# Fifteen tiny router-logit loads on the scalar queue of a two-group top-2 dispatch kernel

## The chip, the cores and the metric

The kernel runs on one core of one Trainium2 chip. The metric is the device time of one execution in microseconds (us), the median over several runs. In the profile, DVE is the vector engine, ACT the scalar engine, POOL GpSimd, and SP the sync engine; SPq and ACTq are the instruction queues from which the sync and scalar engines issue transfers. Sixteen DMA engines move the data for both; q1 holds what SP issued, q10 what ACT issued.

## What is computed

Sixteen batches of 1024 tokens give 16384 rows of 512 float32 numbers. Each row has eight router logits. The softmax over the eight is cut to its two largest, these two are scaled to sum to one, and the row is written twice, once times each weight:

```python
    topk_indices = np.argsort(probs, axis=-1)[..., -k:]
    topk_probs = np.take_along_axis(probs, topk_indices, axis=-1)
    topk_probs = topk_probs / np.sum(topk_probs, axis=-1, keepdims=True)
    x_expanded = x[:, :, np.newaxis, :].repeat(k, axis=2)
    return (x_expanded * topk_probs[..., np.newaxis]).astype(np.float32)
```

Of two logits that differ by d, the weights are sigmoid(-d) and sigmoid(d), so neither exponentials nor a division is needed. The work is almost all movement: 33.6 MB of x in, 67.1 MB out.

## The kernel before, in words

The 16384 rows are laid over 128 partitions, 128 rows in each, and cut in two groups of 65 and 63 rows (`GROUPS`). The tile `xs` has 65 places for rows; `osp` has 18 places for pairs of output rows. Group 0 is loaded in pieces of 6, 28 and 31 rows, group 1 in pieces of 4, 28 and 31 (`LOADS`). Where the text says "28-row load" or "31-row load" it means the one of group 1, unless it says otherwise.

The logits come behind the first piece (lines 144 and 145), and `top2_weights` turns all of them into the weights `WA` by a small tournament on DVE and two sigmoids on ACT. Then each group is multiplied out in the pieces of `STORES`: some into `osp`, others in place, into the part of `xs` whose rows are already used up. The multiplications are DVE passes (line 164), but for the last four rows of group 1's first piece, which ACT makes (line 157). Each piece is stored by line 176.

Loads and stores all go out on SP in the order of the program, but for two on ACT: the first store of group 0, and the 4-row load of group 1, which the text calls the late load. The late load stands behind a pause: line 128 copies two rows onto themselves on ACT, and is made to wait until the fourth of group 0's five stores has landed. The fifth store of group 0 (16 rows out of `xs`) is called the last store below. The 28-row load and the 31-row load follow on SP.

Every transfer reports its landing on one of eight completion counters. The framework deals the counters out in turn in the order of the program, and a transfer that takes a counter again waits, before it is issued, until the transfer that held the counter before has landed. In the program as built before the change the order and the counters are: first load 0, the two logit loads 1 and 2, group 0's 28 rows 3, the store on ACT 4, group 0's 31 rows 5, the other four stores of group 0 on 6, 7, 0 and 1 (the last store has 1), the late load 2, the 28-row load 3, the 31-row load 4, and the four stores of group 1 on 5, 6, 7 and 0. The 28-row load waits for counter 7 (a store that has read the rows it overwrites); the 31-row load waits for counter 1, the last store, for the same reason.

Of the kernel before, what the change touches and what calls it, by code (L numbers as in the profile page):

```python
# [1 line left out]

# [4 lines left out]

F32 = mybir.dt.float32
ALU = mybir.AluOpType
ACTF = mybir.ActivationFunctionType  # L10
P = 128


def top2_weights(nc, WA, dlt, room, logits, E):

    tt = nc.vector.tensor_tensor
    hi, lo, n = None, None, E  # L20
    while n > 1:
        n //= 2
        if hi is None:
            a, b = logits[:, :, 0:n], logits[:, :, n : 2 * n]
            nhi, nlo = room(n), b
            tt(nhi, a, b, op=ALU.max)  # L26
            tt(nlo, a, b, op=ALU.min)  # L27
        else:
            a, b = hi[:, :, 0:n], hi[:, :, n : 2 * n]
            nhi, nlo, tmp = room(n), room(n), room(n)  # L30
            tt(tmp, lo[:, :, 0:n], lo[:, :, n : 2 * n], op=ALU.max)  # L31
            tt(nlo, a, b, op=ALU.min)  # L32
            tt(nlo, nlo, tmp, op=ALU.max)  # L33
            tt(nhi, a, b, op=ALU.max)  # L34
        hi, lo = nhi, nlo
    tt(dlt, hi[:, :, 0], lo[:, :, 0], op=ALU.subtract)  # L36
    nc.scalar.activation(WA[:, :, 0], dlt, ACTF.Sigmoid, scale=-1.0)  # L37
    nc.scalar.activation(WA[:, :, 1], dlt, ACTF.Sigmoid, scale=1.0)  # L38

GROUPS = [65, 63]

LOADS = [[6, 28, 31], [4, 28, 31]]
BASE = [0, 1]

STORES = [
    [(0, 3, "osp", 0), (3, 15, "osp", 3), (18, 16, "xs", 0), (34, 15, "osp", 0), (49, 16, "xs", 33)],
    [(0, 16, "osp", 2), (16, 16, "xs", 0), (32, 15, "osp", 0), (47, 16, "xs", 32)],
]  # L50

L = 18

FREE = [3, 2]

ACT_ROWS = 4


@with_exitstack
def kernel(  # L60
    ctx: ExitStack,
    tc: tile.TileContext,
    x: bass.AP,
    router_logits: bass.AP,
    k: bass.AP,
    out: bass.AP,
):
    nc = tc.nc
    B, S, D = x.shape
    E = router_logits.shape[-1]  # L70
    N = B * S
    assert int(k) == 2 and E == 8 and N == P * sum(GROUPS)
    M = N // P

    x_v, o_v, rl_v = [], [], []
    t0 = 0
    for n in GROUPS:
        t1 = t0 + P * n
        x_v.append(
            x.rearrange("b s d -> (b s) d")[t0:t1].rearrange("(p m) d -> p m d", p=P)  # L80
        )
        o_v.append(
            out.rearrange("b s k d -> (b s) k d")[t0:t1].rearrange(
                "(p m) k d -> p m k d", p=P
            )
        )
        rl_v.append(
            router_logits.rearrange("b s e -> (b s) e")[t0:t1].rearrange(
                "(p m) e -> p m e", p=P
            )  # L90
        )
        t0 = t1

    wpool = ctx.enter_context(tc.tile_pool(name="wpool", bufs=1))
    xs = wpool.tile([P, max(GROUPS), D], F32)
    osp = wpool.tile([P, L, 2, D], F32)
    WA = wpool.tile([P, M, 2], F32)
    dlt = wpool.tile([P, M], F32)


    flat = osp.rearrange("p l k d -> p (l k d)")
    taken = [0]

    def room(n):
        o = taken[0]
        taken[0] += M * n
        return flat[:, o : o + M * n].rearrange("p (m n) -> p m n", n=n)

    logits = room(E)

    def place(where, at, n):

        if where == "osp":
            return osp[:, at : at + n]
        return xs[:, at : at + 2 * n, :].rearrange("p (r k) d -> p r k d", k=2)

    m0 = 0
    stores = []
    for g, G in enumerate(GROUPS):
        x0, r = BASE[g], 0  # L120
        for n in LOADS[g]:

            late = g == 1 and r == 0
            if late:


                rows = xs[:, x0 : x0 + 2, :]
                pause = nc.scalar.activation(rows, rows, ACTF.Copy)  # L128
                tc.add_manual_dep(
                    pause.ins,  # L130
                    stores[-2].ins.name,
                    mybir.DependencyInfo(
                        mybir.DependencyClass.Sync, mybir.DependencyReason.DATA
                    ),
                    reason="begin when the store ahead of the last has landed",
                )
                tc.keep_in_program_order(pause)
            queue = nc.scalar if late else nc.sync
            load = queue.dma_start(xs[:, x0 + r : x0 + r + n, :], x_v[g][:, r : r + n, :])  # L139
            tc.keep_in_program_order(load)  # L140
            r += n
            if g == 0 and r == 6:
                n0 = GROUPS[0]
                tc.keep_in_program_order(nc.sync.dma_start(logits[:, :n0], rl_v[0]))  # L144
                tc.keep_in_program_order(nc.sync.dma_start(logits[:, n0:], rl_v[1]))  # L145
                top2_weights(nc, WA, dlt, room, logits, E)
        assert r == G
        for r, n, where, at in STORES[g]:
            og = place(where, at, n)

            again = where == "osp" and at == 0 and r > 0
            cuts = [0, FREE[g], n] if again else [0, n]
            if g == 1 and r == 0:
                cuts = [0, n - ACT_ROWS]
                for j in range(n - ACT_ROWS, n):
                    for k2 in range(2):
                        nc.scalar.activation(  # L157
                            og[:, j, k2, :],
                            xs[:, x0 + r + j, :],
                            ACTF.Copy,  # L160
                            scale=WA[:, m0 + r + j, k2 : k2 + 1],
                        )
            for a, b in zip(cuts, cuts[1:]):
                nc.vector.tensor_tensor(  # L164
                    og[:, a:b],
                    xs[:, x0 + r + a : x0 + r + b, :]
                    .unsqueeze(2)
                    .to_broadcast([P, b - a, 2, D]),
                    WA[:, m0 + r + a : m0 + r + b, :]
                    .unsqueeze(3)  # L170
                    .to_broadcast([P, b - a, 2, D]),
                    op=ALU.mult,
                )

            queue = nc.scalar if g == r == 0 else nc.sync
            stores.append(queue.dma_start(o_v[g][:, r : r + n], og))  # L176
            tc.keep_in_program_order(stores[-1])
        m0 += G


# [1 line left out]
_INS = ['x', 'router_logits', 'k']  # L182
_OUTS = [((16, 1024, 2, 512), 'float32')]

_NUMBERS = {'k': 2}


# [26 lines left out]
```

## Time and profile before

| what | value |
|---|---|
| median of 3 runs | 239.71 us (239.71 to 239.82) |
| span of the profiled execution | 238.1 us |
| what lies around the span, against the median | 1.6 us |
| bytes moved | 101.19 MB, mean 425 GB/s |
| DVE busy, ACT busy | 137.6 us, 7.9 us |

The profile gives no time of its own for the profiled execution beside its span; the 1.6 us are the median less that span. In the view by windows the columns are the stretch in us from the start of the span, its length, the busy time of DVE, ACT and POOL with their instructions, the granted TensorE clock, the share of the stretch for which the DMA engines were busy, and GB/s. A packet there is counted where it starts, so a share over 1 only means that packets that start in the stretch run on past its end.

### The profile page before, as it was taken

What the parts mean: (1) busy time and instruction counts of PE and PEld (TensorE: products, weight loads), DVE (VectorE), ACT (ScalarE), POOL (GpSimd) and SP (SyncE); (2) the same over time, 40 slices, a digit from 0 to 9 for tenths busy, and PEclk for the clock granted to TensorE, in tenths of its full rate; (3) what the DMA queues carried; (4) which work ended last, traced back from release to release, by engine and by line L of the source; (5) the groups of instructions that cost most, each with busy time, mean ns of one, the idle gap of its engine ahead of it and who ended that gap; (6) DMA issues with size and microseconds to landing.
All of it is one profiled execution on the core that took longest, in us unless ns stands there. A gap on an engine that the chain in (4) does not pass through costs nothing.

```text
span 238.1 us, 115 instructions
## 1 busy us (share of the span) xinstructions
DVE 137.6 (58%) x22; ACT 7.9 (3%) x12; POOL 0.2 (0%) x4
## 2 busy tenths in 40 slices
DVE  0560499999789999100000009999936999950000
ACT  2000000000000000010000007000000000000000
POOL 0000000000000000000000000000000000000000
DMA  7979998979998999989999899898989989979894
GB/s 262 533 337 519 430 418 374 496 341 495 462 396 374 506 433 392 495 352 483 486 396 417 376 479 501 352 506 363 517 363 451 429 363 495 485 341 517 352 528 176
DMA packets 2448, 101.19 MB, mean 425 GB/s; under 512 B 272, under 2 KB 400, under 8 KB 528
## 3 DMA queue, kind: packets, MB, share of 16 engines
q1 hardware_dynamic: 2160, 98.57, 96.1%
q10 hardware_dynamic: 288, 2.62, 2.6%
HBM read 34.08 MB, written 67.11 MB: 425 GB/s over the span
## 4 chain that ended last, share of the span: by engine, by line
DMA 50%; DVE 38%; SPq 1%; issue 0%; DVEq 0%
DMA xs<-in_x_dram 30%; DVE osp L164 24%; DMA out_dram<-osp 20%; DVE xs L164 14%; SPq L144 0%; SPq L145 0%; SPq L139 0%; SPq L176 0%; DVEq L164 0%
## 5 line engine op out<-in xcount | busy, mean ns | idle before, releaser
L164 DVE TENSOR_TENSOR osp<-xs,WA 128x3072 f32<-128x3072 f32 (+4 forms) x7 | 65.1, 9298 | 65.6 <-DMA xs<-in_x_dram 56.8
L164 DVE TENSOR_TENSOR xs<-xs,WA 128x16384 f32<-128x16384 f32 x4 | 68.9, 17225 | 0.2
L157 ACT ACTIVATE osp<-xs,WA 128x512 f32<-128x512 f32 x8 | 5.0, 708 | 37.6 <-DMA xs<-in_x_dram 37.6
L26 DVE TENSOR_TENSOR osp<-osp 128x512 f32<-128x512 f32 x1 | 0.7, 692 | 8.4 <-DMA osp<-in_router_logits_dram 8.4
L128 ACT ACTIVATE xs<-xs 128x1024 f32<-128x1024 f32 x1 | 1.1, 1056 | 90.8 <-DMA out_dram<-osp 90.8
L37 ACT ACT_TABLE_LOAD x1 | 1.3, 1283 | 0.7 <-PEq L195 0.7
L27 DVE TENSOR_TENSOR osp<-osp 128x512 f32<-128x512 f32 x1 | 0.7, 691 | 0.0
L32 DVE TENSOR_TENSOR osp<-osp 128x256 f32<-128x256 f32 (+1 forms) x2 | 0.7, 350 | 0.0
L31 DVE TENSOR_TENSOR osp<-osp 128x256 f32<-128x256 f32 (+1 forms) x2 | 0.7, 350 | 0.0
L33 DVE TENSOR_TENSOR osp<-osp 128x256 f32<-128x256 f32 (+1 forms) x2 | 0.7, 350 | 0.0
L34 DVE TENSOR_TENSOR osp<-osp 128x256 f32<-128x256 f32 (+1 forms) x2 | 0.7, 348 | 0.0
L37 ACT ACTIVATE WA<-dlt 128x128 f32<-128x128 f32 x1 | 0.3, 317 | 10.3 <-DVE dlt L36 10.3
L36 DVE TENSOR_TENSOR dlt<-osp 128x128 f32<-128x128 f32 x1 | 0.3, 292 | 0.0
L38 ACT ACTIVATE WA<-dlt 128x128 f32<-128x128 f32 x1 | 0.3, 299 | 0.0
L195 POOL MEMSET const-bfloat16-1.0<- 128x1 bf16 x1 | 0.1, 102 | 0.0
L195 POOL MEMSET const-uint8-127<- 128x1 uint8 x1 | 0.1, 102 | 0.0
L195 POOL MEMSET const-float32-1.0<- 128x1 f32 x1 | 0.1, 99 | 0.0
L195 POOL MEMSET const-float32-0.0<- 128x1 f32 x1 | 0.1, 98 | 0.2 <-issue 0.2
## 6 DMA issues: line engine op xcount, KB each, us to landing
out_dram<-osp SPq DMA_DIRECT2D x3, 7680.0 KB, 23.4
xs<-in_x_dram SPq DMA_DIRECT2D x2, 7936.0 KB, 40.9
xs<-in_x_dram SPq DMA_DIRECT2D x2, 7168.0 KB, 35.2
xs<-in_x_dram SPq DMA_DIRECT2D x1, 1536.0 KB, 6.2
out_dram<-osp ACTq DMA_DIRECT2D x1, 1536.0 KB, 24.7
xs<-in_x_dram ACTq DMA_DIRECT2D x1, 1024.0 KB, 24.8
osp<-in_router_logits_dram SPq DMA_DIRECT2D x1, 260.0 KB, 6.4
osp<-in_router_logits_dram SPq DMA_DIRECT2D x1, 252.0 KB, 6.6
```

The costliest lines, as they stand in the source:

```text
L26: tt(nhi, a, b, op=ALU.max)
L27: tt(nlo, a, b, op=ALU.min)
L31: tt(tmp, lo[:, :, 0:n], lo[:, :, n : 2 * n], op=ALU.max)
L32: tt(nlo, a, b, op=ALU.min)
L33: tt(nlo, nlo, tmp, op=ALU.max)
L34: tt(nhi, a, b, op=ALU.max)
L36: tt(dlt, hi[:, :, 0], lo[:, :, 0], op=ALU.subtract)
L37: nc.scalar.activation(WA[:, :, 0], dlt, ACTF.Sigmoid, scale=-1.0)
L128: pause = nc.scalar.activation(rows, rows, ACTF.Copy)
L157: nc.scalar.activation(og[:, j, k2, :], xs[:, x0 + r + j, :], ACTF.Copy, scale=WA[:, m0 + r + j, k2 : k2 + 1],)
L164: nc.vector.tensor_tensor(og[:, a:b], xs[:, x0 + r + a : x0 + r + b, :] .unsqueeze(2) .to_broadcast([P, b - a, 2, D]), WA[:, m0 + r + a : ...
L195: nc = _bacc.Bacc("TRN2", target_bir_lowering=False, num_devices=1)
```

## The change

A tile `probe` is added, 15 slots of 20 numbers in each partition. Right behind the late load, fifteen loads are added on the ACT queue. Load number n reads the first 4 + n numbers of each of the first n rows of the router logits, laid as 128 rows of 1024 numbers, into slot n - 1 of `probe`: one row of 20 bytes in the first, fifteen rows of 76 bytes in the last, 120 rows and 6880 bytes in all. Nothing reads `probe`. They are called tiny loads 1 to 15.

```diff
     dlt = wpool.tile([P, M], F32)
+    probe = wpool.tile([P, 15, 20], F32)
...
             queue = nc.scalar if late else nc.sync
             load = queue.dma_start(xs[:, x0 + r : x0 + r + n, :], x_v[g][:, r : r + n, :])
             tc.keep_in_program_order(load)
+            if late:
+                rows2 = router_logits.rearrange("b s e -> (b s e)").rearrange(
+                    "(p m) -> p m", p=P
+                )
+                for n2 in range(1, 16):
+                    w = 4 + n2
+                    tc.keep_in_program_order(
+                        nc.scalar.dma_start(probe[:n2, n2 - 1, :w], rows2[:n2, :w])
+                    )
```

In the program as built the instructions of DVE, POOL and PE stay as they were, and so do SP's transfers and their order. On ACT the fifteen loads stand between the late load and the eight copies of line 157. In the program's order they stand ahead of the 28-row and the 31-row load, so they take fifteen turns of the counters: tiny loads 1 to 7 have counters 3, 4, 5, 6, 7, 0 and 1, tiny load 8 has 2, tiny loads 9 to 15 have 3 to 7, 0 and 1. The 28-row load now has counter 2, the 31-row load 3, and the four stores of group 1 have 4 to 7. The waits for the holder before are, as built:

| transfer | queue | counter | waits for |
|---|---|---|---|
| tiny load 1, 2, 3, 4 | ACT | 3, 4, 5, 6 | transfers of group 0 ahead of its last three stores |
| tiny load 5, 6 | ACT | 7, 0 | nothing more (the pause has waited for both) |
| tiny load 7 | ACT | 1 | the last store |
| tiny load 8 | ACT | 2 | the late load |
| tiny loads 9 to 15 | ACT | 3 to 7, 0, 1 | tiny loads 1 to 7 |
| 28-row load | SP | 2 | tiny load 8, and counter 7 as before |
| 31-row load | SP | 3 | tiny load 9, and the last store as before |
| stores of group 1 | SP | 4 to 7 | tiny loads 10 to 13, and what they waited for before |

The eight copies of line 157 and the first DVE pass of group 1 wait for the 28-row load under its new counter.

## Prediction

> **What bounds the kernel now.** I read the page's busy slices and queues first, then the chain of waits, then the timeline around the late load.
>
> ```profile
> DVE 137.6 (58%) x22; ACT 7.9 (3%) x12; POOL 0.2 (0%) x4
> ...
> DMA  7979998979998999989999899898989989979894
> ...
> DMA packets 2448, 101.19 MB, mean 425 GB/s; under 512 B 272, under 2 KB 400, under 8 KB 528
> ...
> q1 hardware_dynamic: 2160, 98.57, 96.1%
> q10 hardware_dynamic: 288, 2.62, 2.6%
> ```
>
> The DMA engines are the bound: 96.1% + 2.6% of their time is taken, no slice stands below 7 but the tail, and DVE has 42% to spare. What leaves the engines empty anywhere in the middle therefore comes out at the end. What merely adds bytes costs next to nothing when the bytes are 6880 of 101 million.
>
> ```profile
> 96.78 45.47 DMA xs<-in_x_dram
> 142.25 0.03 issue
> 142.27 0.05 DVEq L164
> 142.32 0.04 issue
> 142.37 12.97 DVE osp L164
> ...
> 194.61 17.23 DVE xs L164
> ```
>
> In the chain of waits the 28-row load is issued at 96.78 and holds the chain until 142.25, when the first DVE pass of group 1 is let go. All that ends the program hangs on that landing.
>
> ```profile
> 96.39 0.33 SPq L176 DMA_DIRECT2D out_dram<-xs  x1
> 96.78 28.30 SPq L139 DMA_DIRECT2D xs<-in_x_dram  x2
> 103.64 1.06 ACT L128 ACTIVATE xs<-xs 128x1024 f32<-128x1024 f32 x1 [90.84 <-DMA out_dram<-osp]
> 104.73 0.34 ACTq L139 DMA_DIRECT2D xs<-in_x_dram  x1
> 142.32 5.01 ACT L157 ACTIVATE osp<-xs,WA 128x512 f32<-128x512 f32 x8 [37.62 <-DMA xs<-in_x_dram]
> 142.37 12.96 DVE L164 TENSOR_TENSOR osp<-xs,WA 128x12288 f32<-128x12288 f32 x1 [46.00 <-DMA xs<-in_x_dram]
> ```
>
> The timeline shows why the early issue matters. The last store goes out at 96.39, the 28-row load 0.4 us later, long before the store's data have left: its data lie in the queue behind the store's. The 31-row load, the second of the two in the 28.30, had to wait for the last store to land:
>
> ```profile
> SPq L139 <- DMA out_dram<-xs: 26.9, 1, 26.9
> ...
> L139 SPq DMA_DIRECT2D xs<-in_x_dram x5: 340/441/965, 0.7 to 124.7; - x5
> ```
>
> The last issue of that line starts at 124.7, so that is when the last store's landing is known. The late load is known to have landed 24.8 us (its row of DMA issues, below) after 104.73, at 129.5.
>
> **The change part by part.** Added are fifteen issues on ACT, 120 rows, and a changed dealing of the counters. Three things have to be priced.
>
> *The issues.* ACT issues the late load in 0.34 us; the five of SP on line 139 take 0.340 to 0.965. Fifteen take 5.1 us by the first figure, 14.5 by the last. ACT has nothing to do from 105.07 until 142.32 (37.62 idle in the row above), so the issuing as such is hidden; without that cover it would cost those 5 to 14 us.
>
> *The rows.* Three stretches of the DMA view, after the last store's final packets, price small packets:
>
> ```profile
> DMA packets 64, 1.18 MB, mean 590 GB/s; under 512 B 16, under 2 KB 16, under 8 KB 16
> ...
> q1 hardware_dynamic: 32, 0.92, 106.2%
> q10 hardware_dynamic: 32, 0.26, 30.9%
> ...
> q1 hardware_dynamic: 16, 0.92, 68.3%
> q10 hardware_dynamic: 16, 0.13, 10.0%
> ...
> q1 hardware_dynamic: 16, 0.92, 264.5%
> q10 hardware_dynamic: 16, 0.00, 1.1%
> ```
>
> They are 123.5 to 125.5, 125.5 to 128.6 and 128.6 to 129.4. In the last, 16 packets on 16 engines fill 1.1% of 0.8 us: 9 ns for a completion packet. The 16 of 57,344 bytes beside them take 264.5% of 0.8 us, 2.12 us each. The busiest engine gets at most 15 tiny rows and 15 completions; at 9 ns that is 0.3 us, and it is spread over a stretch in which the engines are empty anyway, as comes next. I take 0, at most 0.3.
>
> *The waits.* This decides. The 28-row load now waits on SP for tiny load 8; tiny load 8 stands on ACT behind tiny load 7, which waits for the last store, and itself waits for the late load. So the 28-row load can't be issued at 96.8 any more, but only when the last store and the late load have landed and a tiny load has made its round trip. By then q1 and q10 are empty. Behind the waiting instruction on SP stand the 31-row load and all of group 1's stores; for them wait DVE, and ACT with line 157. Behind tiny load 7 on ACT stand tiny loads 8 to 15 and the eight copies.
>
> Step by step, in us from the start:
>
> 1. Last store known landed: 124.7. Its path before that is untouched. Tiny load 7 is issued, 0.34, until 125.1.
> 2. Late load landed. The three stretches show q1 and q10 taking turns packet by packet: between the last store's 16 completions (first stretch, under 512 B) and the late load's own (third stretch) each engine served two packets of the 28-row load. Without them the late load is done 2 x 2.12 = 4.2 earlier: 129.5 - 4.2 = 125.3.
> 3. Tiny load 8 is issued from 125.3 and has to come back. The trace has no tiny load, so I bound it:
>
> ```profile
> 0.73:1.73 1.00, 0.00 (x0) 1.00 (x1) 0.00 (x0) 1.00 0.00 0
> 1.73:2.73 1.00, 0.00 (x0) 0.28 (x1) 0.00 (x0) 1.00 1.08 221
> 2.73:4.73 2.00, 0.00 (x0) 0.00 (x0) 0.00 (x0) 1.00 0.98 406
> ...
> xs<-in_x_dram SPq DMA_DIRECT2D x1, 1536.0 KB, 6.2
> out_dram<-osp ACTq DMA_DIRECT2D x1, 1536.0 KB, 24.7
> xs<-in_x_dram ACTq DMA_DIRECT2D x1, 1024.0 KB, 24.8
> osp<-in_router_logits_dram SPq DMA_DIRECT2D x1, 260.0 KB, 6.4
> ```
>
> The first load of the program, issued at 0.73 into empty queues, has no packet for 1.0 us. The late load's completions start within 128.6 to 129.4, and its landing is known at 129.5; I take 0.4 for the telling, between 0.1 and 0.9. So at least 1.4. From above: the 1.57 MB of the first load take 3.7 us at 425 GB/s, and it landed after 6.2, so 2.5 at most if nothing is odd about small rows. I take 2.0, in the middle: the packet is small, but the first ones of an empty queue are slow (221 GB/s in the second row against 406). SP is let go at 127.3.
> 4. The 28-row load is issued into empty queues: first packet 1.0 later, 128.3. The slow start of the second row costs (1 - 221/406) of a microsecond, 0.5.
> 5. Eight packets of 2.12 us on each engine are 16.9; with 0.4 for the telling of the landing and 0.3 of spread between the engines, 128.3 + 0.5 + 16.9 + 0.7 = 146.4, against 142.25. The 28-row load lands 4.2 us late.
> 6. The 31-row load waits for tiny load 9, issued one step behind tiny load 8, and goes out some 0.5 us behind the 28-row load, whose data take 17: hidden. Tiny loads 10 to 13 were issued by about 127.5, and the stores that now wait for them come after 155: hidden. ACT has its tiny loads out by 128 or 129, ahead of the copies.
>
> From 142.25 on nothing is known to take the delay up:
>
> ```profile
> 142.25:172.00 29.75, 29.54 (x2) 5.01 (x8) 0.00 (x0) 1.00 0.96 415
> 172.00:212.00 40.00, 34.09 (x4) 0.00 (x0) 0.00 (x0) 1.00 1.01 436
> ```
>
> The engines are full at 0.96 and 1.01, and every pass and store there hangs on the two loads. The idle share is 0.04 x 29.75 = 1.2 us, so even if all of it were reclaimed 3 would stay. Sum: 238.1 + 4.2 = 242.3 of span, with the 1.6 around it 243.9; from the median, 239.71 + 4.2 = 243.9 too.
>
> Ends of the range: with 1.4 for the round trip and no slow start, 4.2 - 0.6 - 0.5 = 3.1, so 242.8. With 2.5, and with tiny loads 7 and 8 issued at 0.965 instead of 0.34, 4.2 + 0.5 + 1.2 = 5.9, so 245.6.
>
> The Trainium skill, page "DMA: Bandwidth & Descriptors", section "Anatomy of one DMA", gives a fixed cost of about 2.0 us per transfer, most of it the receipt of the last byte (stated for transfers from GpSimd); its estimate for step 3 would be 2.0, inside the 1.4 to 2.5 of the rows.
>
> **The rivals.**
>
> *No hold: the tiny loads cost only their issue.* If the 28-row load went out at 96.8 as before, all is hidden behind ACT's 37.62 of idle time and 0.3 us of packets: 239.7 to 240.0. For it speaks that nothing reads what the tiny loads bring, and that they stand on another queue. Against it: SP's transfer shares a counter with tiny load 8 in the built order. The same page, section "Issuing engines are not separate DMA queues", says that another issuing engine only saves sequencer time as all share 16 engines, which would make this change free; the turn-taking of q1 and q10 above agrees with the sharing, but the rule leaves the wait out.
>
> *Not slower: the release comes while the last store still fills the engines.* Place: the wait of the 28-row load on SP. If tiny load 8's landing were told by about 122.5 (the first packet of the 28-row load needs 1.0, and the last store's packets run out 0.4 before 124.7), q1 would never run dry, and the late load would only change turns with another queue entry: 239.7. That is the point from which it decides. Against it stands that tiny load 7 ahead of it waits for the last store's landing, at 124.7, so it would need the counters to be told early.
>
> *A dearer round trip.* The smallest loads in the trace, the logits, took 6.4. They stood behind the first load's 1.57 MB, but if 6.4 were the price of a load of small rows as such, step 3 grows by 4.4: 239.71 + 8.6 = 248.3. The 9 ns packets speak against it.
>
> **How the numbers follow.** The hold with one short round trip 0.86, no hold 0.04, early release 0.03, dear round trip 0.07. The time is that of the first, 243.9. Its own bounds are 242.8 to 245.6; for what the steps may have left out I add 0.4 on each side, 242.4 to 246.0, which leaves the rivals out. A measurement of this kernel tells 0.2%, 0.48 us, from no change. The two rivals at 239.7 give "within" most of their 0.07, "faster" 0.02 as packets may fall into place a little better; the rest, 0.92, is slower.
>
> **What would show it.** In the chain of waits after, the 28-row load starts near 127 instead of 96.78, behind a tiny load into `probe` on ACT; SP's longest wait on the loads' line is then for that. The busy slices of DMA dip once, near slice 21 (125 to 128.5), and the first pass of group 1 starts near 146.5, its idle time 50 instead of 46.00. The late load's landing time falls from 24.8 to about 20.6. It is wrong if the 28-row load is still issued near 97, if the empty stretch lasts over 5 us, or if the shift at the first pass of group 1 isn't found again at the end.

## The result and the profile after

| | before | after |
|---|---|---|
| median | 239.71 us (239.65 to 239.82, 4 runs) | 245.25 us (244.94 to 246.31, 4 runs) |
| span of the profiled execution | 238.1 us | 243.6 us |
| first DVE pass of group 1 begins | 142.37 us | 146.66 us |

The ratio is 1.023, 95% interval 1.0204 to 1.0257: slower by 5.5 us, where 4.2 were forecast. The median lies inside the stated range. The lines below are from the page of the changed kernel: its span, the busy share of the DMA engines in 40 slices, the bytes per slice, and the two queues.

```profile
span 243.6 us, 130 instructions
...
DMA  7999999998997979979958997999898989989894
GB/s 262 534 452 366 431 398 481 380 484 353 465 517 344 506 323 484 495 344 404 565 178 339 452 458 344 500 334 495 366 495 366 495 366 485 444 373 495 366 495 183
...
q1 hardware_dynamic: 2160, 98.57, 94.8%
q10 hardware_dynamic: 528, 2.63, 2.6%
```

q1 carries the same packets and bytes as before, in a longer span. q10 has 240 packets more, twice the 120 rows, so one completion to each row, and still 2.6%. The one thing that stands out is the 5 in the 21st slice, at 178 GB/s: the engines run dry once. The chain of waits of the changed kernel names the place:

```profile
104.70 20.55 DMA xs<-in_x_dram
125.25 0.02 issue
125.27 1.24 DMA probe<-in_router_logits_dram
126.50 0.02 issue
126.52 20.02 DMA xs<-in_x_dram
146.54 0.03 issue
146.56 0.05 DVEq L174
146.61 0.04 issue
146.66 12.97 DVE osp L174
159.63 0.02 SPq L186
159.65 0.03 issue
159.68 26.34 DMA out_dram<-osp
186.02 0.02 issue
186.04 14.04 DVE osp L174
```

Late load, tiny load 8, 28-row load, one after the other: the tiny load, which nobody reads, is a link of the chain. The 28-row load is issued at 126.52 instead of 96.78. The list of what SP's queue waited for (us in total, times, longest) says the same of the changed kernel:

```profile
SPq L140 <- DMA probe<-in_router_logits_dram: 29.8, 1, 29.8
```

and its timeline shows fifteen issues that stretch over 23 us on ACT, as they stop at tiny load 7, and SP's two loads right behind tiny load 8:

```profile
105.08 23.28 ACTq L149 DMA_DIRECT2D probe<-in_router_logits_dram  x15
126.52 0.81 SPq L140 DMA_DIRECT2D xs<-in_x_dram  x2
```

The view by windows of the changed kernel, last two columns share and GB/s:

```profile
124.45:125.10 0.65, 0.00 (x0) 0.00 (x0) 0.00 (x0) 1.00 0.17 52
125.10:127.30 2.20, 0.00 (x0) 0.00 (x0) 0.00 (x0) 1.00 0.02 1
```

From 125.10 to 127.30 the engines are busy for 2% of the time. In the kernel before, where the 28-row load had long been issued, the same view has no such gap:

```profile
125.00:130.00 5.00, 0.00 (x0) 0.00 (x0) 0.00 (x0) 1.00 0.91 393
```

The first pass of group 1 comes 146.66 - 142.37 = 4.29 us later, but the span is 243.6 - 238.1 = 5.5 us longer. So another 1.2 us arise after that pass. In the chain they lie between the issue of group 1's first store and its landing, 26.34 us here. In the kernel before:

```profile
155.40 25.13 DMA out_dram<-osp
```

The DMA view of the packets that start just ahead of that store's data shows where they went. Each stretch holds the last packet of the 31-row load on each of the 16 engines; for the kernel before it is 157.7 to 158.4:

```profile
DMA packets 16, 1.02 MB, mean 1451 GB/s; under 512 B 0, under 2 KB 0, under 8 KB 0
...
q1 hardware_dynamic: 16, 1.02, 356.0%
```

and for the changed kernel 161.6 to 162.6:

```profile
DMA packets 16, 1.02 MB, mean 1016 GB/s; under 512 B 0, under 2 KB 0, under 8 KB 0
...
q1 hardware_dynamic: 16, 1.02, 343.1%
```

The share is that of 16 engines over the stretch, so share times length is the mean time of a packet: 356.0% of 0.7 us is 2.49 us before, 343.1% of 1.0 us is 3.43 us after. The same 63,488 bytes take 0.94 us more in the mean of the engines. The packet that starts last takes 2.58 us before (80.8% of the 0.2 us from 158.2) and 3.77 after (235.8% of the 0.1 us from 162.5): on the engine that is done last the difference is the whole 1.2 us. The prediction had no such term.

### The profile page after: what moved, and what is told of

Read it like the earlier page. It is cut to its first block, busy times and chain, and to the rows that moved or that the text cites. A ratio compares the mean times of both kernels' runs of the same rounds, so it can differ in the third digit from the quotient of the medians.

```text
span 243.6 us, 130 instructions
## 1 busy us (share of the span) xinstructions
DVE 137.6 (57%) x22; ACT 7.9 (3%) x12; POOL 0.2 (0%) x4
## 4 chain that ended last, share of the span: by engine, by line
DMA 58%; DVE 30%; SPq 1%; ACT 0%; issue 0%; DVEq 0%; ACTq 0%
DMA out_dram<-osp 30%; DMA xs<-in_x_dram 27%; DVE osp L174 23%; DVE xs L174 7%; DMA probe<-in_router_logits_dram 1%; ACT xs L129 0%; SPq L155 0%; SPq L154 0%; SPq L140 0%; DVEq L174 0%; ACTq L129 0%; SPq L186 0%
```

## The experiments

Two things were to be told apart: whether the hold on the 28-row load costs (theory A) or the tiny rows do (rival B), and what the extra 1.2 us are. Differences are against the kernel before on the same chip, whose median was 239.90 in the first four, 239.83 in the next four, 239.87 in the last two.

**Five tiny loads.**

```diff
-                for n2 in range(1, 16):
+                for n2 in range(1, 6):
```

> Five tiny loads instead of fifteen: the 28-row load takes counter 0, whose holder (a store) lands near 103, so it is released at about 103.6, twenty us before the last store's data have left; the 31-row load waits only for the last store, as before. If the hold is what costs (theory A): 239.5 to 240.2 us, the first pass of group 1 near 142.5, no empty stretch. If tiny rows on the scalar queue cost by themselves, for instance by delaying single engines or by the 1.2 us seen after 146 (rival B): 240.3 to 241.2, since five of fifteen are kept.

Measured: 239.97 us, ratio 0.9997 (0.9977 to 1.0016). The timeline has the 28-row load issued at 103.56, and the first pass begins where it did:

```profile
103.56 21.51 SPq L140 DMA_DIRECT2D xs<-in_x_dram  x2
...
105.09 5.21 ACTq L149 DMA_DIRECT2D probe<-in_router_logits_dram  x5
142.31 12.96 DVE L174 TENSOR_TENSOR osp<-xs,WA 128x12288 f32<-128x12288 f32 x1 [45.95 <-DMA xs<-in_x_dram]
```

Seven us of hold cost nothing here: the engines had the last store's data to move meanwhile, and their share from 104 to 122 is 1.03 in this profile as in the one before. Five tiny loads cost nothing that can be told either, though ACT spent 5.2 us on issuing them.

**Seven tiny loads.** The same edit with `range(1, 8)`.

> Seven tiny loads: the 28-row load takes counter 2 and waits for the late load itself, no longer for tiny load 8. Theory A: it is issued near 125.3 instead of 126.5, so the first pass of group 1 comes 1.2 earlier than with fifteen, near 145.4, and the time is 245.25 - 1.2 = 244.0 (243.6 to 244.5). Rival B (the tiny rows cost, not the hold): about half of the loss goes with half of the rows, 242.5.

Measured: 244.65 us, ratio 1.019 (1.0172 to 1.0208). Theory A had asked for 243.6 to 244.5 and is missed by a little; rival B, at 242.5, by much. Seven tiny loads have 28 of the 120 rows, not half of them, so rival B should even have asked for about 241.2. The late load was known to have landed at 125.86 in this profile, not at 125.25, and the 28-row load was issued at once:

```profile
125.86 0.02 issue
125.88 20.23 DMA xs<-in_x_dram
146.11 0.03 issue
146.14 0.05 DVEq L174
146.19 0.04 issue
146.23 12.97 DVE osp L174
```

One packet of the last store, starting at 121.75, took 2.90 us here where the others of its size take 2.42; that is most of the 0.6 by which the late load is later. Why it was slow isn't shown.

**The hold without any tiny load.** In the kernel before:

```diff
             load = queue.dma_start(xs[:, x0 + r : x0 + r + n, :], x_v[g][:, r : r + n, :])
+            if g == 1 and r == 4:
+                tc.add_manual_dep(
+                    load.ins,
+                    before.ins.name,
...
+                    reason="begin when the late load has landed",
+                )
             tc.keep_in_program_order(load)
+            before = load
```

> No tiny load at all; the 28-row load is made to wait for the late load. Theory A with the extra 1.2 us behind 146 belonging to the hold (a load started into empty queues): as with seven tiny loads, 244.0 (243.5 to 244.5), last packets of the 31-row load over 3 us. If the extra 1.2 belongs to the tiny loads: 242.8, last packets of the 31-row load as before, 2.4 to 2.6 us. Rival B: 239.7.

Measured: 244.63 us, ratio 1.0192 (1.0174 to 1.0211), as with seven tiny loads to 0.02 us. Theory A's 243.5 to 244.5 is missed by 0.13; here too the late load was late, known at 125.84, with one slow packet of the last store (3.13 us, starting at 121.50). Not one tiny row is needed for this loss of 4.73 us; what fifteen lose beyond it goes with a later release, at 126.52. The chain has the 28-row load behind the late load:

```profile
104.65 21.19 DMA xs<-in_x_dram
125.84 0.02 issue
125.86 20.07 DMA xs<-in_x_dram
```

The last packets of the 31-row load are stretched here as well (160.7 to 162.1, the same DMA view):

```profile
q1 hardware_dynamic: 16, 1.02, 245.4%
```

245.4% of 1.4 us is 3.44 us. So the extra belongs to the hold, not to the tiny rows.

**All fifteen on GpSimd's queue**, the first made to wait for the pause, so that they run at about the same time (issued from 105.0 to 140.5):

```diff
-                    tc.keep_in_program_order(
-                        nc.scalar.dma_start(probe[:n2, n2 - 1, :w], rows2[:n2, :w])
-                    )
+                    tiny = nc.gpsimd.dma_start(probe[:n2, n2 - 1, :w], rows2[:n2, :w])
+                    if n2 == 1:
...
+                            reason="begin when the pause is over",
+                        )
+                    tc.keep_in_program_order(tiny)
```

> All fifteen tiny loads, issued by GpSimd from about 104.7 on, where they take no turn of the eight counters of SP and ACT. The 28-row load is issued near 96.8 again. Theory A: 239.5 to 240.2. Rival B: the rows are the same and so is the time, 244 to 245; if only the 1.2 us belongs to the rows, 240.9.

Measured: 240.92 us, ratio 1.0038 (1.0026 to 1.005). The same rows, with no turn of the counters taken: 4.5 us of the 5.5 are gone, and the 28-row load is issued at 96.83 again. The forecast of no loss is missed by 0.7, and 240.9, the forecast for "only the 1.2 us belongs to the rows", is hit. The hold alone, above, speaks against that reading, as it has the extra with no row at all; and of the 1.0 us in the span here, 0.13 are there at the first pass (142.50), 0.39 more at the first store's landing (25.52 instead of 25.13), and the other half comes behind the issue of the last store. Yet the last packets of the 31-row load are stretched a little here as well (157.9 to 158.6):

```profile
q1 hardware_dynamic: 16, 1.02, 408.8%
```

408.8% of 0.7 us is 2.86 us, with no hold and no empty stretch before. So a part of the stretch can come without empty queues. Why GpSimd's loads, which made 480 packets (q0) of the 120 rows, cost this wasn't followed up.

**Six tiny loads.** `range(1, 7)`; the 28-row load waits for the last store alone.

> Six tiny loads: the 28-row load takes counter 1 and waits for the last store alone, landing near 124.7; the late load's last packets are then still to come. If the loss is set by when the 28-row load is let go (theory A): issued at 124.7 to 125.3, 0.6 to 1.2 us ahead of the two kernels that wait for the late load (125.9), so 243.4 to 244.1 against their 244.64. If the price is one of any hold at all, whenever it ends (rival): 244.6.

Measured: 243.56 us, ratio 1.0158 (1.0145 to 1.0172); theory A's 243.4 to 244.1 holds. The chain has the 28-row load behind the last store:

```profile
96.39 28.31 DMA out_dram<-xs
124.71 0.02 issue
124.72 19.92 DMA xs<-in_x_dram
```

Put beside the others, the loss follows the time of release. The first four columns are of the profiled execution; the last is the difference of the medians of all runs. The profiled executions of the two kernels that wait for the late load were the slowest of their runs, so their spans show more than their medians do.

| released at | by | first pass later by | span longer by | median longer by |
|---|---|---|---|---|
| 96.78 | (before) | 0 | 0 | 0 |
| 103.56 | a store of group 0 | -0.06 | 0.0 | 0.07 |
| 124.72 | the last store | 2.46 | 3.5 | 3.73 |
| 125.86 | the late load (hold alone) | 3.69 | 5.1 | 4.73 |
| 125.88 | the late load (seven) | 3.86 | 5.4 | 4.75 |
| 126.52 | tiny load 8 | 4.29 | 5.5 | 5.54 |

From 124.72 on each us of delay moves the first pass by about one us, and behind that pass another 1.0 to 1.6 us are lost. But a release at the very landing of the last store already costs 3.5 us of span: that much comes with starting the 28-row load into empty queues, before any wait for the late load or a tiny load is added.

**One load in place of fifteen.**

```diff
-                for n2 in range(1, 16):
...
+                tc.keep_in_program_order(
+                    nc.scalar.dma_start(probe[:15, 0, :19], rows2[:15, :19])
+                )
```

> One load of 15 rows of 19 numbers in place of the fifteen; it takes one turn of the counters, so the 28-row load has counter 4, whose holder landed long before. Theory A: no hold, 28-row load near 96.8, 239.6 to 240.2, the same as before within 0.2%. If small rows on the scalar queue held single engines up: 240.3 or more.

Measured: 239.78 us, ratio 0.9999 (0.9991 to 1.0008). It takes one turn of the counters; the 28-row load goes out at 96.71. It brings 15 x 19 numbers, which hold all that the fifteen brought, and costs nothing that can be measured.

**What stretches the last packets?** First guess: the store that arrives while they run. Two kernels move that store, by changing how many rows ACT makes. With the hold of the third experiment:

```diff
-ACT_ROWS = 4
+ACT_ROWS = 6
```

> No tiny loads; the 28-row load waits for the late load as in the hold without tiny loads (244.63), and ACT makes six rows of group 1's first piece instead of four, so that its first store is issued some 2.2 us earlier, near 157, about 3.9 ahead of the last packets of the 31-row load instead of 1.7. Theory G, the last packets are stretched (3.0 to 3.9 us instead of 2.34) because the store comes to the engines while those packets run: they are back to 2.34 to 2.6 and the time falls by about 1, to 243.6. Theory S, they are stretched because the sixteen engines run out of step after a start into empty queues: still 3.0 to 3.9, 244.6.

and in the kernel before, without a hold:

```diff
-ACT_ROWS = 4
+ACT_ROWS = 3
```

> The kernel before with no hold, but ACT makes three rows instead of four, so that the first store of group 1 is issued 1.1 us later, near 156.5, 1.4 ahead of the last packets of the 31-row load instead of 2.4. Theory G (the store's coming sets the stretch): the last packets take over 3 us and the time rises by about 1, to 240.7. Theory S (engines out of step): packets of 2.34 to 2.6 and 239.7 to 239.9.

Measured: 243.96 us, ratio 1.0173 (1.0158 to 1.0189), and 239.78, ratio 1.0001 (0.9992 to 1.001). The last packets of the 31-row load in the DMA view, with the hold (159.9 to 161.2):

```profile
q1 hardware_dynamic: 16, 1.02, 272.9%
```

and without (157.7 to 158.4):

```profile
q1 hardware_dynamic: 16, 1.02, 340.4%
```

These are 3.55 us with the hold though the store came 3.9 us ahead of them, and 2.38 without, though it came only 1.4 ahead. Moving the store by 1 to 2 us neither took the stretch away nor brought it about; theory G falls. The time with the hold fell by 0.7 all the same, between the two forecasts: in the profiled execution the late load was known at 125.15 and the 28-row load issued at 125.17, 0.7 earlier than in that of the third experiment.

**A store between the two loads**, to tell engines out of step from something that is paid once. With the hold, and without it:

```diff
             r += n
+            if g == 1 and r == 32:
+                tc.keep_in_program_order(
+                    nc.sync.dma_start(o_v[0][:, 34:36], osp[:, 0:2])
+                )
```

> Hold without tiny loads, and a store of 1 MB (two rows of group 0 written a second time with the same numbers) between the 28-row and the 31-row load; the bytes alone add 2.5 us, so 244.6 + 2.5 = 247.1 in either theory. Theory S (the sixteen engines are out of step and every switch from loads to a store suffers): the last packets of the 31-row load are stretched as before, 3.0 to 3.9 us instead of 2.34. Theory P (a stream of loads that starts into empty queues pays about 1 us once, where the first store follows it): the stretch moves to the last packets of the 28-row load, near 143 (over 2.9 us instead of 2.12), and those of the 31-row load are at 2.34 to 2.7.

> The same store between the two loads in the kernel before, with no hold: 239.8 + 2.5 = 242.3 in both theories, and no packet of either load over 2.7 us: the stretch needs the empty queues. If a store between two loads costs by itself, the 28-row load's last packets are stretched here too.

Measured: 246.57 us with the hold, ratio 1.0279 (1.0257 to 1.0301); 242.55 without, ratio 1.011 (1.0095 to 1.0125). The forecasts were 247.1 and 242.3; with the hold it is missed by 0.5. The DMA view with the hold, first the last packets of the 28-row load (141.5 to 142.7), then those of the 31-row load (163.6 to 164.9):

```profile
q1 hardware_dynamic: 16, 0.92, 266.2%
...
q1 hardware_dynamic: 16, 1.02, 180.2%
```

and the 28-row load's last packets without the hold (139.3 to 140):

```profile
q1 hardware_dynamic: 16, 0.92, 319.3%
```

266.2% of 1.2 us is 3.19 us where other packets of this size take 2.12: the stretch has moved to the load ahead of the inserted store. 180.2% of 1.3 us is 2.34 for the 31-row load: none is left there, although the engines still start these packets up to 1.1 us apart. Without the hold the 28-row load's last packets take 2.24, and the 31-row load's 2.37 (197.1% of the 1.2 us from 160.2). So theory P fits and S falls: with the hold, about 1 us per engine is paid once, where the first store follows the loads.

That empty queues alone bring it isn't shown. In GpSimd's run some 0.4 us of it (2.86 against 2.49) came without them. And at the program's start, where loads also go into empty queues, the last packets of group 0's 28-row load (23.1 to 23.8, in the kernel before) take 355.7% of 0.7 us, 2.49 instead of 2.12, so 0.4 and not 1; there the store on ACT's queue takes turns with them. What in the engines does this stays open; the traces give only the packets' times.

## Why the prediction was right, and what it missed

The steps, by their numbers in the prediction:

1. and 2. The last store is known landed as before, and the late load at 125.25, forecast 125.3: the two turns less for the 28-row load were the right account.
3. The round trip of tiny load 8 took 1.24 us (125.27 to 126.50 in the chain), below the 1.4 to 2.5 of the bounds and the 2.0 taken. Both terms of the lower bound, which came from loads with rows of 8 and 12 KB, were too long for this one with rows of 48 bytes: the first packet came 0.87 us after the issue began (at 126.14), not 1.0, and the landing was told 0.3 us after the last completion packet (126.21), not 0.4. The Trainium skill, page "DMA: Bandwidth & Descriptors", section "Anatomy of one DMA", gives about 2.0 us as the fixed cost of a transfer, for another issuing path; the measured 1.24 decides here.
4. and 5. From its issue the 28-row load needed 20.02 us, where the prediction had 1.0 + 0.5 + 16.9 + 0.7 = 19.1. The first packets on the 16 engines, those that start from 127.45 to 128.8, took 207.8% of 1.35 us, 2.81 each against 2.12,

```profile
q1 hardware_dynamic: 16, 0.92, 207.8%
```

so the slow start is 0.7 in the mean, where 0.5 was taken. The missing 0.9 is the spread: these packets began up to 1.2 us apart, and the prediction had taken 0.3 for the engines' spread from no row. The engine that began last, 2.19 us after the issue, needed 2.66 for its first packet (83.1% of the 0.2 us from 128.6) and 2.12 for each of the other seven, and 0.37 went into the telling: 20.02 in sum. This error and that of step 3 nearly cancel, so the shift at the first pass was 4.29, forecast 4.2. That it agrees so well is luck.

6. The tiny loads behind number 8, the 31-row load and the stores were hidden, as forecast. So were the issues: the first six took 5.0 us on ACT (105.08 to 110.10), at most 1.11 each, and those from tiny load 7 on 0.28 to 0.45 each. The rows cost nothing that can be told, as forecast: seven loads with 28 rows came to 244.65, the hold without any to 244.63. No run has all fifteen on ACT's queue without the hold.

The step that failed is the account behind 142.25. The prediction asked whether later idle time could take the delay up, and found rightly that it couldn't; it didn't ask whether the hold costs a second time. It does: 0.94 us in the mean of the last packets ahead of the first store, 1.2 us in the span. With this term the sum is 4.3 + 1.2 = 5.5, as measured. One of the prediction's own signs of being wrong, that the shift at the first pass isn't found again at the end, thus came true, with 4.3 against 5.5. The time lies inside its bounds of 242.8 to 245.6 all the same, but their upper end had been worked out from a longer round trip and longer issues, and neither was there. The mechanism, the hold on the 28-row load by tiny load 8, was right; that the range held is partly luck.

Of the rivals, "no hold" was what five tiny loads and the one load measured, 239.97 and 239.78; as a forecast for this change it fell, since SP did wait. The early release fell with SP's 29.8 us of waiting, until 126.52. The dearer round trip fell with the 1.24.

## What to carry to other kernels

A transfer costs more than its bytes where completion counters are dealt out in turn: each one more moves the dealing, and a large load may find itself waiting for a small one on another queue. Read from the built program which transfer each large load waits for, and count small transfers or merge them, as here, where one load of 15 rows was free, five loads too, and six, seven and fifteen cost 3.7, 4.8 and 5.5 us. A queue that feeds a bandwidth-bound kernel must not run dry: a wait was free here while the data ahead of it still flowed (7 us of hold cost nothing), and one that ended only with their landing cost 3.7 us, plus about its further length.

## What the runs showed of the hardware that was not expected

A stream of loads held until the queues were empty paid twice: its first packets of 57,344 bytes took 2.81 us instead of 2.12 and began up to 1.2 us apart, and the last packets ahead of the next store took 3.43 instead of 2.49. When a store was put between the two loads, the second price moved to the packets ahead of that store (3.19 instead of 2.24). And fifteen tiny loads on GpSimd's queue, 480 packets, cost 1.0 us with no hold at all; about half of that came behind the issue of the last store. On ACT's queue five loads (15 rows) couldn't be told from none.
